# A per-row factor on VectorE: one operation with a scalar operand, or two multiplications of columns

## The chip, the cores and the metric

The kernel runs on one core of a Trainium2 chip. The metric is the time of one execution on the device, in microseconds (us), lower being better. Engines are named as in the profile: PE (TensorE), with its weight loads as PEld, DVE (VectorE), ACT (ScalarE), POOL (GpSimd) and SP (the engine that issues most transfers).

## The reference, cut to what matters

One encoder layer on 1024 tokens of width 1024: a combined projection, differential attention and a state-space mixer side by side, an output projection with a layer norm, and a mixture of 32 experts with a second layer norm. The change touches the differential attention alone. Each of its 4 heads has two softmax distributions over the same keys, and the second is taken from the first with a factor:

```python
sc = jnp.einsum('bqhcd,bkhcd->bhcqk', qi, k).astype(jnp.float32) * scale
p = jax.nn.softmax(sc, axis=-1)
attn = p[:, :, 0] - lam * p[:, :, 1]
return jnp.einsum('bhqk,bkhe->bqhe', attn.astype(v.dtype), v)
```

Then follow a root-mean-square norm over each head's 128 outputs and a gain.

## The kernel before, in words

**Stages.** The first stage makes the projections (line 244) beside the state-space mixer (`ssm_prepare`, `ssm_unit`). The second is attention, a loop over 32 units; woven into it are the gate of the mixer (`glu`, line 733), the splitting of the output weights (`wo_part`, line 877) and, at its end, preparations for routing. The third is the output projection (`mix`, line 1077) over 8 blocks of 128 tokens, with the layer norm (`layernorm`) and routing (`route`). The fourth is the experts (lines 1237 and 1246), and the fifth the second norm.

**A unit of attention** is one head `h` and one block `i` of 128 queries; it has `n = 128 * (i + 1)` keys. `scores` (line 771) makes the two score matrices on PE (lines 780 and 781), masks 64 rows with a MEMSET (789 or 797), takes the negated maximum `nm` with a reduction on DVE (790 or 798), and forms the exponentials `p` on ACT with their sums into `L` (783). `L` has two columns for a unit, one for each distribution. `weigh` (line 802) then takes the reciprocals `RL` of both sums (805), makes the column `rho` (807), which has one number for each query, and adds `rho` times the second distribution to the first, in place in `p` (808). PE transposes the result (814), ACT or DVE copies it to `half` (815), and PE multiplies it with the values (818). The first distribution's own normalizing factor cancels in the norm, up to its epsilon, and is put in by `normalize` (line 821) through small multiplications of `ss` with `RL` on DVE (830, 831 and 834, shown under helper line 158), a power on POOL (833) and a product on POOL (835).

**The order of work.** The loop starts unit `u + 2` before it weighs unit `u`. Up to the first gather of the experts, a planner puts the traced instructions in order for each engine by its own estimates of when they are ready, so DVE's queue is not in the order of the code: reductions of a later unit stand between the steps of an earlier one. From that gather on (`pins`, line 1387) `keep_order` keeps each engine's order as traced. Each engine runs its own queue strictly in order. The tile `rho` comes from `sm` (line 754), which has four buffers of one column.

**What POOL does meanwhile.** It subtracts the rounded part of a tensor from the tensor, in pieces of 64 or 128 partitions by 1024 with two operands (the `split` helper's line 155; `queries`, line 764), for `ql`, `zl`, `wgl` and `wol`; it scales the gate (line 738, shown as helper line 170, on `wg_raw`); and it runs the power and the product of `normalize`.

**Helpers.** Many DVE instructions are recorded under the line of a helper: `mul` is 158, `sub` 155, `stt` (scalar_tensor_tensor, one operation with a scalar operand and a second one with a tensor) 164, and `ts` (tensor_scalar) 168 or 170. `nlam`, a column of 128 equal numbers, is made once, early (lines 408 to 410).

Of the kernel before, what the change touches and what calls it, by code (L numbers as in the profile page):

```python
# [16 lines left out]
ALU = mybir.AluOpType  # L17
# [97 lines left out]
def tile_kernel(ctx: ExitStack, tc: tile.TileContext, I: dict, out: bass.AP, dbg=None):  # L115
# [15 lines left out]
    def bank(name, which=0):  # L131

        if which == 1:
            turn[0] ^= 1
            which = 2 + turn[0]
        return psum.tile([P, 512], F32, tag=f"bank{which}", name=name, bufs=1 if which else 2)
# [20 lines left out]
    def mul(out_, a, b, eng=V):  # L157
        eng.tensor_tensor(out=out_, in0=a, in1=b, op=ALU.mult)  # L158
# [4 lines left out]
    def stt(out_, a, s, b, op0, op1):  # L163
        return V.scalar_tensor_tensor(out=out_, in0=a, scalar=s, in1=b, op0=op0, op1=op1)  # L164
# [243 lines left out]
    nlam = cp.tile([P, 1], F32, name="nlam")  # L408
# [345 lines left out]
    def sm(name, n, bufs=4):  # L754
        return cp.tile([P, n], F32, tag=name, name=name, bufs=bufs)
# [46 lines left out]
    def weigh(h, i, p_, L, RL, j, po):  # L802

        n = P * (i + 1)
        V.reciprocal(RL[:, j, :], L[:, j, :])
        rho = sm("rho", 1)
        stt(rho, L[:, j, 0:1], nlam, RL[:, j, 1:2], ALU.mult, ALU.mult)
        stt(p_[:, 0, 0:n], p_[:, 1, 0:n], rho, p_[:, 0, 0:n], ALU.mult, ALU.add)
        aT = half.get("aT", [8, P], bufs=2)
        for k0 in range(0, i + 1, 4):  # L810
            k1 = min(k0 + 4, i + 1)
            b_ = bank(f"at{h}_{i}_{k0}")
            for k in range(k0, k1):
                PE.transpose(b_[:, (k - k0) * P:(k - k0 + 1) * P], p_[:, 0, k * P:(k + 1) * P], ident)
            (V.tensor_copy if k0 else S.copy)(aT[:, k0:k1, :], b_[:, 0:(k1 - k0) * P].rearrange("p (k q) -> p k q", q=P))  # L815
        sl.put(p_)
        for k in range(i + 1):
            PE.matmul(po[:, j * P:(j + 1) * P], aT[:, k, :], vv[k // 4][:, k % 4, h * P:(h + 1) * P],  # L818
                      start=(k == 0), stop=(k == i))
# [74 lines left out]
    for u, (h, i) in enumerate(units):  # L894
        if u + LEAD < len(units):
            start(u + LEAD)
        L_, RL_, po_ = grp[h, i // 4]
        weigh(h, i, live.pop(u), L_, RL_, i % 4, po_)
        if u in late:
            late.pop(u)()  # L900
        ends[h, i // 4] = ends.get((h, i // 4), 0) + 1
        if ends[h, i // 4] == 4:
            late[u + LATE] = normalize(h, i // 4, po_, RL_)
        if u in fills:
            for f_, *a_ in fills[u]:
                {"ask": ask, "pre": glu_prepare, "glu": glu, "wo": wo_part}[f_](*a_)
        if u == ZERO:

            zero = sl.get([P, D], F32, "zero")
            G.memset(zero, 0.0)  # L910
            for j in range(4):
                SP.dma_start(moe_dram[512 * j:512 * j + 512, :].rearrange("(p a) n -> p a n", p=P),
                             zero.unsqueeze(1).broadcast_to([P, 4, D]))
# [703 lines left out]
```

## Time and profile before

| What | us |
|---|---|
| median of 3 runs | 1185.71 |
| lowest and highest of them | 1184.47, 1189.87 |
| the profiled execution, its own time | 1182.18 |
| its span in the trace | 1180.4 |
| DVE busy over the span | 970.2 |
| POOL busy over the span | 359.0 |

The span is the stretch between the first and the last instruction of the trace; 1.8 us of the profiled execution's own time lie around it. The profiled execution is 3.5 us below the median of the other runs, so a sum made on its rows is set against 1182.18 and then carried to the median.

To read the rows: a timeline row gives start, duration, engine, line, operation, the tile written and those read, shapes and a count; a duration reaches from the instruction's start on its engine to its end, so an instruction held up by something after it has started shows a long duration, not idle time. The chain of waits is the work that ended last, followed back from the end; a piece of it is the time that one group of instructions held the chain.

### The profile page before, as it was taken

Reading aid. Unit: us, or ns where it says so; the run is one execution under the profiler, and the core shown is the slowest. Engines: PE = TensorE matmul, PEld = TensorE weight load, DVE = VectorE, ACT = ScalarE, POOL = GpSimd, SP = SyncE. Lnnn points to the kernel's source line nnn. Section 1 sums busy time; section 2 is a strip of 40 time slices with the busy share of each in tenths; the row PEclk is TensorE's granted clock in tenths of the full one; section 3 lists DMA queues with packets and bytes.
Section 4 is the critical chain, followed back from the end, with each engine's and each line's share of the span. In section 5 each row is a group of like instructions: output and inputs, shape, how many; then the busy total and the mean of one; then the engine's idle time right before and its main releaser. Section 6 shows DMA issues by size and latency. Waiting matters only on the chain.

```text
span 1180.4 us, 15229 instructions
## 1 busy us (share of the span) xinstructions
PE 1081.9 (92%) x5345; PEld 902.0 (76%) x5345; DVE 970.2 (82%) x1430; ACT 711.6 (60%) x960; POOL 359.0 (30%) x297
## 2 busy tenths in 40 slices
PE   6979999896779899995999999999999999999983
PEld 4867887686668788884888888888888888888852
DVE  4898666657878874565999999999999999999955
ACT  3312333445656743213888888888888888888832
POOL 1087464422442643341212122122122122121122
PEclk9989999998999999995999999999999999999997
DMA  8531111211181454545699999999999999999582
GB/s 208 138 99 43 55 46 46 59 30 42 32 325 36 159 210 136 196 178 200 238 361 378 383 369 399 383 385 396 381 374 376 377 370 386 395 386 386 172 208 108
DMA packets 90622, 278.90 MB, mean 236 GB/s; under 512 B 29404, under 2 KB 49900, under 8 KB 66096
## 3 DMA queue, kind: packets, MB, share of 16 engines
q1 hardware_dynamic: 78016, 252.78, 57.1%
q0 software_dynamic: 11520, 24.83, 7.7%
q8 instruction: 43, 0.70, 0.2%
q10 hardware_dynamic: 1008, 0.30, 0.1%
q14 instruction: 35, 0.29, 0.1%
HBM read 254.12 MB, written 34.60 MB: 245 GB/s over the span
## 4 chain that ended last, share of the span: by engine, by line
PE 74%; DVE 13%; ACT 5%; DMA 3%; issue 3%; SPq 1%; POOL 1%; ACTq 0%; DVEq 0%; POOLq 0%
PE g L1246 15%; PE u L1246 14%; PE y L1237 14%; PE proj L244 8%; PE mix L1077 7%; PE xT L1207 3%; DMA misc<-in_w_in_dram 2%; ACT p L783 2%; PE glu L733 2%; PE po L818 1%; PE hT L1219 1%; PE x L1449 1%; PE pl L1099 1%; DVE ssmt L158 1%; DVE ssm L158 1%
## 5 line engine op out<-in xcount | busy, mean ns | idle before, releaser
L1146 POOL DMA_INDIRECT moe_dram<-yo,idx x30 | 52.1, 1738 | 425.9 <-DVE yo L164 425.9
L244 PE MATMUL proj<-xh,wa 128*128 128x512 f32 x256 | 75.9, 403 | 1.7 <-ACT ssm L678 1.6
L244 PE MATMUL proj<-xh,wb 128*128 128x512 f32 x256 | 73.9, 400 | 1.6 <-ACT ssm L678 1.6
L1077 PE MATMUL mix<-woh,mx 128*128 128x512 f32 x256 | 74.3, 401 | 0.7 <-ACT p L783 0.7
L1141 POOL DMA_INDIRECT gx<-h_dram,idx x32 | 60.2, 1881 | 22.5 <-DVE WT L161 13.1
L783 ACT ACTIVATE p<-s,nm 128x1024 f32<-128x1024 f32 (+7 forms) x64 | 47.3, 745 | 26.8 <-DVE nm L798 17.0
L244 PEld LDWEIGHTS proj<-xh,wa 128*128 128x128 f32 x256 | 48.6, 193 | 11.8 <-ACT ssm L678 1.8
L244 PEld LDWEIGHTS proj<-xh,wb 128*128 128x128 f32 x256 | 48.0, 191 | 11.4 <-ACT ssm L678 1.8
L1077 PEld LDWEIGHTS mix<-woh,mx 128*128 128x128 f32 x256 | 48.1, 191 | 10.5 <-ACT p L783 1.0
L1253 ACT ACTIVATE yo<-y,WT 128x1024 f32<-128x1024 f32 (+1 forms) x33 | 36.0, 1091 | 24.4 <-PE y L1237 24.4
L780 PE MATMUL s<-kk,qh 128*128 128x512 f32 (+3 forms) x96 | 38.0, 399 | 12.5 <-ACT p L783 12.2
L818 PE MATMUL po<-vv,half 128*128 128x128 f32 x288 | 43.4, 294 | 6.7 <-ACT half L815 6.6
L818 PEld LDWEIGHTS po<-vv,half 128*128 128x128 f32 x288 | 39.2, 205 | 9.9 <-ACT half L815 8.7
L1207 PEld LDWEIGHTS xT<-ident,gx 128*128 128x128 f32 x256 | 36.2, 208 | 9.9 <-DMA gx<-h_dram,idx 5.8
L1207 PE MATMUL xT<-ident,gx 128*128 128x128 f32 x256 | 36.9, 287 | 7.0 <-DMA gx<-h_dram,idx 5.6
L155 DVE TENSOR_TENSOR xe<-xT,xe 128x1024 fp32r<-128x1024 f32 (+1 forms) x33 | 39.2, 1189 | 4.3 <-ACT xe L174 4.3
L244 PE MATMUL proj<-xl,wa 128*128 128x512 f32 x128 | 42.6, 404 | 0.0
L164 DVE SCALAR_TENSOR_TENSOR yo<-gx,first,yo 128x1024 f32<-128x1024 f32 (+1 forms) x33 | 41.3, 1252 | 1.5
L1077 PE MATMUL mix<-wol,mx 128*128 128x512 f32 x128 | 42.2, 398 | 0.0
L244 PE MATMUL proj<-xl,wb 128*128 128x512 f32 x128 | 41.4, 399 | 0.0
L174 ACT CAST xe<-xT 128x1024 fp32r<-128x1024 f32 (+1 forms) x33 | 32.3, 979 | 13.6 <-PE xT L1207 13.6
L164 DVE SCALAR_TENSOR_TENSOR p<-p,rho 128x1024 f32<-128x1024 f32 (+7 forms) x32 | 36.2, 1135 | 1.0 <-DMA moe_dram<-zero 0.3
(864 smaller groups left out, 3546.7 us busy)
## 6 DMA issues: line engine op xcount, KB each, us to landing
misc<-in_w_in_dram SPq DMA_DIRECT2D x16, 512.0 KB, 3.9
moe_dram<-zero SPq DMA_DIRECT2D x4, 2048.0 KB, 13.2
xr<-in_x_dram SPq DMA_DIRECT2D x8, 512.0 KB, 8.5
wo_raw<-in_w_out_dram SPq DMA_DIRECT2D x4, 1024.0 KB, 4.8
xa<-in_x_dram SPq DMA_DIRECT2D x8, 512.0 KB, 3.5
h_dram<-xa SPq DMA_DIRECT2D x8, 512.0 KB, 3.2
mo<-moe_dram SPq DMA_DIRECT2D x8, 512.0 KB, 6.0
mo<-moe_dram POOLq DMA_DIRECT2D x8, 512.0 KB, 13.1
```

Of the source, the lines that this page charges most:

```text
L155: eng.tensor_tensor(out=out_, in0=a, in1=b, op=ALU.subtract)
L164: return V.scalar_tensor_tensor(out=out_, in0=a, scalar=s, in1=b, op0=op0, op1=op1)
L244: PE.matmul(o[:, hs], wt[kt // 4][:, w_, kt % 4, :], x_[:, hs], start=(kt == 0 and n == 0), stop=(kt == KT - 1 and n == 2))
L780: PE.matmul(s_[:, c0:c0 + w], qd[0][:, c, tk], kk[h][:, c, c0:c0 + w], start=True, stop=False)
L783: S.activation(p_[:, c, 0:n], s_[:, 0:n], AF.Exp, bias=nm[:, c:c + 1], accum_out=L[:, j, c:c + 1])
L818: PE.matmul(po[:, j * P:(j + 1) * P], aT[:, k, :], vv[k // 4][:, k % 4, h * P:(h + 1) * P], start=(k == 0), stop=(k == i))
L1077: PE.matmul(o[-(hs.start > 0)][:, hs], mx[:, m_, kt, :], (woh, wol)[w_][kt // 2][:, kt % 2, hs], start=(kt == 0 and n == 0), stop=(kt == K ...
L1141: return G.indirect_dma_start(out=dst, out_offset=None, in_=h_dram[:, :], in_offset=bass.IndirectOffsetOnAxis(ap=ix, axis=0), bounds_check ...
L1146: G.indirect_dma_start(out=moe_dram[:, :], out_offset=bass.IndirectOffsetOnAxis(ap=ix, axis=0), in_=src, in_offset=None, bounds_check=2 * ...
L1207: PE.transpose(b_[:, kt * P:(kt + 1) * P], rows(g_, kt), ident)
L1237: PE.matmul(y[h_], hid[e][:, x_, kt, :], w_[:, k, HALVES[h_]], start=(kt == 0 and n == 0), stop=(kt == 3 and n == 2))
L1246: PE.matmul(o, xT[e][:, x_, kt, :], w_[:, k, :], start=(kt == 0 and n == 0), stop=(kt == KT - 1 and n == 2))
```

## The change

The factor `rho = L0 * nlam * RL1` of each unit was one scalar_tensor_tensor on DVE, which takes the column `L0`, multiplies it with the scalar operand `nlam` and then with the column `RL1`. It becomes two tensor_tensor multiplications, the second in place and dependent on the first. Nothing else is edited; the loop runs it 32 times.

```diff
         V.reciprocal(RL[:, j, :], L[:, j, :])
         rho = sm("rho", 1)
-        stt(rho, L[:, j, 0:1], nlam, RL[:, j, 1:2], ALU.mult, ALU.mult)
+        mul(rho, L[:, j, 0:1], RL[:, j, 1:2])
+        mul(rho, rho, nlam)
         stt(p_[:, 0, 0:n], p_[:, 1, 0:n], rho, p_[:, 0, 0:n], ALU.mult, ALU.add)
```

## Rows read from the trace of the kernel before

**Rows 1.** Windows: stretch, length; busy us (instructions) of PE, PEld, DVE, ACT, POOL; clock, DMA.

```profile
262.00:425.00 163.00, 134.45 (x790) 116.30 (x789) 133.41 (x260) 102.01 (x214) 69.53 (x53) 0.93 0.36 123
425.00:1180.00 755.00, 715.58 (x3381) 592.25 (x3379) 654.31 (x775) 521.93 (x605) 173.13 (x138) 0.98 0.83 315
```

**Rows 2.** Chain of waits from 262 to 450 us, shares by line.

```profile
by line: PE mix L1077 17.6%; ACT p L783 10.9%; PE glu L733 10.1%; PE po L818 8.7%; PE s L780 6.4%; issue 5.7%; DVE p L164 5.7%; PE s L781 5.2%; DVE nm L798 4.2%; DVE rho L164 4.0%; PE at L814 3.3%; ACT half L815 2.9%; DVE nm L790 2.1%; ACT 
```

**Rows 3.** Chain of waits in order of time, pieces: start us, us, what.

```profile
276.26 0.07 DVE rho L164
...
312.58 2.63 DVE rho L164
...
315.23 3.17 DVE p L164
```

**Rows 4.** Groups of DVE instructions by line, attention: count, busy us and mean ns.

```profile
L164 DVE SCALAR_TENSOR_TENSOR rho<-L,nlam,RL 128x1 f32<-128x1 f32 x32 | 13.8, 434 | 0.6
...
L158 DVE TENSOR_TENSOR ss<-ss,RL 128x4 f32<-128x4 f32 x18 | 3.1, 175 | 1.2 <-POOL ss L833 1.2
```

**Rows 5.** Timeline of DVE: an undisturbed unit, and two small multiplications.

```profile
307.46 0.22 DVE L158 TENSOR_TENSOR ss<-ss,RL 128x4 f32<-128x4 f32 x2
...
319.56 0.15 DVE L805 RECIPROCAL RL<-L 128x2 f32<-128x2 f32 x1
319.75 0.22 DVE L164 SCALAR_TENSOR_TENSOR rho<-L,nlam,RL 128x1 f32<-128x1 f32 x1
320.01 0.48 DVE L164 SCALAR_TENSOR_TENSOR p<-p,rho 128x256 f32<-128x256 f32 x1
```

**Rows 6.** Waits between engines in attention: total us, times, longest.

```profile
ACT p L783 <- DVE nm L798: 17.0, 10, 3.7
...
PE at L814 <- DVE p L164: 3.8, 2, 2.6
```

**Rows 7.** Timelines of POOL and DVE around 372 us, and an undisturbed scaling.

```profile
361.86 0.62 POOL L170 TENSOR_SCALAR wg_raw<-wg_raw 128x512 f32<-128x512 f32 x1 [9.56 <-ACT wg_raw L737]
...
370.23 4.84 POOL L155 TENSOR_TENSOR zl<-zT,zh 128x1024 fp32r<-128x1024 f32 x2 [0.72 <-PE at L814]
375.05 1.32 POOL L170 TENSOR_SCALAR wg_raw<-wg_raw 128x512 f32<-128x512 f32 x1
```

```profile
371.89 0.87 DVE L164 SCALAR_TENSOR_TENSOR rho<-L,nlam,RL 128x1 f32<-128x1 f32 x1
372.79 3.10 DVE L164 SCALAR_TENSOR_TENSOR p<-p,rho 128x768 f32<-128x768 f32 x1
...
376.04 0.82 DVE L798 TENSOR_REDUCE nm<-s 128x1 f32<-128x640 f32 x1
```

**Rows 8.** Timeline of DVE and POOL at the end of attention.

```profile
406.22 4.74 POOL L155 TENSOR_TENSOR wol<-wo_raw,woh 128x1024 fp32r<-128x1024 f32 x2 [0.59 <-ACT woh L174]
...
408.27 0.40 DVE L164 SCALAR_TENSOR_TENSOR rho<-L,nlam,RL 128x1 f32<-128x1 f32 x1
...
408.77 2.46 DVE L164 SCALAR_TENSOR_TENSOR p<-p,rho 128x256 f32<-128x256 f32 x1
...
410.90 0.20 POOL L970 MEMSET route<- 128x128 bf16 x1
411.07 4.70 POOL L155 TENSOR_TENSOR wol<-wo_raw,woh 128x1024 fp32r<-128x1024 f32 x2
411.16 2.34 DVE L168 TENSOR_SCALAR route<-iof 128x32 f32<-128x32 f32 x1
...
413.82 0.42 DVE L790 TENSOR_REDUCE nm<-s 128x2 f32<-128x256 f32 x1
...
416.19 5.06 POOL L155 TENSOR_TENSOR wol<-wo_raw,woh 128x1024 fp32r<-128x1024 f32 x2
```

**Rows 9.** Chain of waits, pieces at the start of the output projection and of the experts.

```profile
415.14 7.26 PE mix L1077 x23
...
545.17 4.43 DMA gx<-h_dram,idx
```

## The prediction

> **What bounds the kernel now.** I read the busy times by stage first. In attention, 163 us long, PE and DVE are each busy for some 134 us, neither of them throughout; behind it PE is busy for 716 of 755 us [rows 1]. So attention is the stage in which DVE can set the end, and what is lost there is carried on: from 415 us the chain of waits runs on PE's output projection, then over routing and the gather of tokens into the experts [rows 9]; I find no idle stretch that would give a loss back.
>
> Next the chain of waits between 262 and 450 us, by line. It changes hands all the time; `rho` holds 4.0% of it, 7.5 us of 188 [rows 2]. In order of time `rho` stands there in 7 of the 32 units, at 276, 280, 288, 313, 333, 372 and 408 us; the first is a piece of 0.07 us, the longest of 2.63 us [rows 3]. That spread is the point. Undisturbed, `rho` takes 0.22 us [rows 5], yet the mean over 32 is 434 ns [rows 4]: 32 x (0.434 - 0.22) = 6.8 us of its 13.8 us are waiting that shows as duration.
>
> What it waits for is seen when DVE and POOL are laid beside each other. From 370.23 us POOL runs two subtractions with two operands, 4.84 us in all, so 2.42 us each. `rho` starts at 371.89 and ends at 372.76, when the first is over; `p` starts at 372.79 and ends 3.10 us later, after the second is over at about 375.07 [rows 7]. Around 408 us the same pair of steps meets the same kind of pair [rows 8]. So an instruction of DVE with two operands that comes during such a subtraction is held until it ends, gets through at the seam, and the next one on DVE is held by the next subtraction.
>
> **The change, step by step.** Removed: 32 scalar_tensor_tensor on one column. Added: 64 tensor_tensor on one column. No transfer, semaphore of another engine or buffer is added, and POOL, ACT and PE issue what they issued.
>
> *The plain cost.* From `rho`'s start to `p`'s it is 0.26 us (319.75 to 320.01), and from `RL`'s start to its dependent `rho` 0.19 us for an instruction of 0.15 us [rows 5]. The nearest row for a small multiplication is `ss`, 18 of mean 175 ns, about 0.15 us where nothing holds it [rows 4]. A dependent one should then take 0.19 us from start to start, as after `RL`, so two take 0.38 in place of 0.26: **+0.12 us a unit**. Lower bound: two `ss` multiplications that do not need each other take 0.22 us together [rows 5], so 0.22 in place of 0.26, -0.04. Upper bound: each multiplication as dear as the old `rho`, 0.52 in place of 0.26, +0.26. I take +0.12, since the second multiplication does need the first. Over the 7 units on the chain that is 0.8 us (bounds -0.3 and +1.8). For the other 25 I take nothing: what covers it is that `p` is made ahead of need, as PE's transposes waited for `p` only twice in the stage [rows 6]. Without that cover it would be 25 x 0.12 = 3.0 us.
>
> [...] With 32 x 0.12 us on the path everywhere that would be 3.8 us; the chain, with 7 units, gives 0.8.
>
> *One more seam.* Where POOL runs two subtractions in a row, `rho` now passes the first seam as its first multiplication, the second multiplication is held in `p`'s place, and `p` comes after the pair. That alone costs little, as `p` had to wait for the end of the pair anyway. It costs where POOL has something next. The chain has two such places.
> - At 375.05 the scaling of `wg_raw` is next. It took 1.32 us because `p` was ahead of it; by itself it takes 0.62 [rows 7]. Now the second multiplication takes that seam and the scaling comes before `p`. **+0.6 us**, bounds 0 (`p` still slips in ahead) and 0.62. Queued behind `p` on DVE are a mask and `nm` of the next unit, for which ACT waits.
> - At 408 us POOL runs six subtractions, with only a MEMSET of 0.20 us at 410.90 between the second and the third, which starts at 411.07 [rows 8]. Now the first multiplication passes at about 408.6, the second at about 410.95, and `p` is ready 0.19 us later, at 411.14: 0.07 us after the third has begun. `p` is then held for 4.70 / 2 = **2.35 us**. Behind it on DVE stand the TENSOR_SCALAR on `iof`, which in the trace of before is held for one subtraction too (2.34 us), and then `nm` at 413.82; ACT's exponentials wait for that, and PE's first output projection at 415.14 for those [rows 8, 9]. Everything there moves by one subtraction. Bounds 0 (the 0.07 us go the other way) and 4.7 (`iof` misses a further seam).
>
> The other contacts (288, 308, 313 and 333 us) have a pause or a transfer of POOL's behind the pair, and one at 389 us lies off the chain: nothing but the plain cost.
>
> The sum is 0.8 + 0.6 + 2.4 = 3.8 us, bounds -0.3 and 1.8 + 0.6 + 4.7 = 7.1. The profiled execution would go from 1182.18 to 1186.0, and the median, 3.5 us above it, from 1185.71 to **1189.5**. That is +0.32%, below the 0.5% (5.9 us) that a measurement of this kernel can tell from no change.
>
> [...]
>
> **The rivals.**
> - *Hidden.* `p` gets in before the third subtraction. For it: a margin of 0.07 us, worked out from starts in one execution. Against it: `p` cannot start before the second multiplication is done, and POOL needs nobody. Time: 0.8 + 0.6 = 1.4, so 1187.1.
> - *Slower: a further seam missed.* Place: the six subtractions from 406.22 us, where DVE's queue holds `p`, `iof` and then the subtractions for the output projection. Each two-operand step that shifts behind one more of POOL's costs 2.35 us. It decides once one more than forecast is missed on the chain: 3.8 + 2.35 = 6.2 us, 1191.9; with two 1194.2, with three 1196.6. For it: POOL runs back to back there. Against it: only three of the six are left by then, and POOL's work isn't made longer, so later steps find it idle sooner.
> - *Faster: the planner's order changes.* It orders DVE by estimates, and the extra step leaves it a gap between the two multiplications, or before `p`. If it puts the next unit's `nm` there, which does not read what POOL holds, ACT gets on while `rho` and `p` would be held. For it: ACT waited 17.0 us for `nm` in 10 waits [rows 6], and at 372 us `nm` came 4.15 us after `rho` had started [rows 7], at 313 us it was 2.63 + 3.17 us of the chain [rows 3]. Both together give -9.9 + 1.4 = -8.5, so 1177.2; one of them only stays within 0.5%. Against it: the planner need not know of POOL's hold, and `nm` was not put there where a gap was open before.
> - *The change does nothing.* If the two multiplications overlapped as freely as the `ss` pair, 0.22 for 0.26 us, the sum is between -0.3 and 0: 1185.7. They are dependent, so this is a small part of the hidden case.
>
> **How the numbers follow.** Chances: forecast 0.36; hidden, with no cost at all among it, 0.24; slower 0.26, as an order that shifts can add holds as well as take them away; faster 0.14. The first two lie within 0.5%: faster 0.14, same 0.60, slower 0.26. The range takes in the forecast, the hidden case and the slower one up to three missed seams (1196.6), and at its low end the sum's lower bound with one of the two gains of the faster case (1185.71 - 0.3 - 4.15 = 1181.3): **1181 to 1197**. Left out are two gains at once and worse orders.
>
> **What would show it.** Right: two TENSOR_TENSOR on `rho` for each unit, about 0.15 us each and 0.19 us apart where POOL is idle; DVE with 32 instructions more; where POOL subtracts in pairs, the long durations sit on both multiplications and `p` is short; at the end of attention `p` is held once more, and the first output projection starts about 3.8 us later. Wrong: `nm` in other places between the steps, an output projection that starts earlier or at the same time, or a difference that arises behind 425 us, where nothing was edited.

## The result, and the profile after

The changed kernel takes 1193.15 us (median of 20 runs, 1188.99 to 1195.74); the kernel before, run beside it, 1184.85 us (20 runs). The ratio is 1.0066 with an interval of 1.0055 to 1.0077, so the change costs **7.8 us**. Forecast were 3.8 us, which would have lain below the 0.5% at which the prediction draws the line for "same" (0.60 of its chances); the measured 0.66% is "slower", which had 0.26. The profiled execution after took 1190.73 us, its span is 1189.0 us.

The windows by stage of the kernel after, to be read beside [rows 1] (stretch, length, busy us and instructions of PE, PEld, DVE, ACT, POOL, clock, DMA):

```profile
262.00:425.00 163.00, 127.81 (x755) 109.01 (x754) 130.29 (x277) 97.33 (x200) 67.27 (x51) 0.92 0.34 111
425.00:1180.00 755.00, 725.38 (x3423) 600.25 (x3421) 655.28 (x792) 526.37 (x620) 178.31 (x140) 0.98 0.84 317
```

Up to 425 us PE has done 35 instructions fewer than before (755 for 790) and ACT 14 fewer; they now lie behind 425 us. Two pieces of the chain of waits, in order of time, answer to [rows 9]:

```profile
426.24 6.08 PE mix L1078 x20
...
552.56 4.36 DMA gx<-h_dram,idx
```

The output projection starts 11.1 us later than at 415.14, the first gather 7.4 us later than at 545.17, and the end of the span is 8.6 us later, so 3.7 us are won back between projection and gather, and behind the gather 1.2 us are added (635.2 us to the end before, 636.4 after). The first unit's `p` starts at 274.65 before and at 275.69 after, so 1.0 of these lay ahead of the first `p`. **First `p` to first gather** is the measure used for all runs below: 270.52 us before, 276.87 after, +6.4.

Groups of DVE instructions by line of the kernel after (count, busy us, mean ns), beside [rows 4]:

```profile
L158 DVE TENSOR_TENSOR rho<-L,RL 128x1 f32<-128x1 f32 x32 | 12.3, 386 | 0.6
L158 DVE TENSOR_TENSOR zT<-zT,wg_raw 128x512 f32<-128x512 f32 x8 | 11.6, 1451 | 0.8 <-POOL wg_raw L170 0.7
L158 DVE TENSOR_TENSOR rho<-rho,nlam 128x1 f32<-128x1 f32 x32 | 7.1, 224 | 0.5
```

The same view of the kernel before has this for the products on `zT`:

```profile
L158 DVE TENSOR_TENSOR zT<-zT,wg_raw 128x512 f32<-128x512 f32 x8 | 5.4, 677 | 0.0
```

Two things are to be seen. The waiting on `rho` sits mostly on the first multiplication (386 ns in the mean for 0.16 us of work), little of it on the second (224 ns), where the forecast had it on both (in the old order, run 1 below, it is on both: 389 and 428 ns). And eight products that the diff does not touch now take 11.6 us instead of 5.4. Both come from one cause, as runs 1 and 2 below show: the planner has put the work in another order, up to the first gather. Against the trace of before, at least 15 instructions of POOL, 50 of ACT, 278 of PE and, beside the 32 new ones, 108 of DVE would have to be moved to get the new order. In 4 of the 32 units an `nm` now stands between the two multiplications, in none of run 1; the prediction had named that as a sign of being wrong. The pair of POOL's subtractions for `wgl`, before and after:

```profile
332.03 4.69 POOL L155 TENSOR_TENSOR wgl<-wg_raw,wgh 128x1024 fp32r<-128x1024 f32 x2
```

```profile
357.78 4.91 POOL L155 TENSOR_TENSOR wgl<-wg_raw,wgh 128x1024 fp32r<-128x1024 f32 x2 [6.04 <-ACT wgh L174]
```

The timeline of DVE where nothing is in the way shows the plain cost:

```profile
371.57 0.15 DVE L805 RECIPROCAL RL<-L 128x2 f32<-128x2 f32 x1
371.76 0.16 DVE L158 TENSOR_TENSOR rho<-L,RL 128x1 f32<-128x1 f32 x1
371.96 0.16 DVE L158 TENSOR_TENSOR rho<-rho,nlam 128x1 f32<-128x1 f32 x1
372.15 0.88 DVE L164 SCALAR_TENSOR_TENSOR p<-p,rho 128x640 f32<-128x640 f32 x1
```

From `RL` to `p` it is 0.58 us, against 0.45 in [rows 5]: +0.13 a unit, where 0.12 were forecast. The timelines of DVE and POOL at the end of attention answer to [rows 8]:

```profile
414.12 4.86 POOL L155 TENSOR_TENSOR wol<-wo_raw,woh 128x1024 fp32r<-128x1024 f32 x2 [0.65 <-ACT woh L174]
...
414.53 2.23 DVE L164 SCALAR_TENSOR_TENSOR p<-p,rho 128x256 f32<-128x256 f32 x1
416.69 2.84 DVE L158 TENSOR_TENSOR zT<-zT,wg_raw 128x512 f32<-128x512 f32 x1
...
419.09 2.64 POOL L155 TENSOR_TENSOR wol<-wo_raw,woh 128x1024 fp32r<-128x1024 f32 x1
...
419.64 2.11 DVE L158 TENSOR_TENSOR rho<-L,RL 128x1 f32<-128x1 f32 x1
421.69 0.29 POOL L972 TENSOR_SCALAR_AFFINE_SELECT route<-route 128x128 bf16<-128x128 bf16 x1
421.78 0.21 DVE L158 TENSOR_TENSOR rho<-rho,nlam 128x1 f32<-128x1 f32 x1
...
421.96 2.33 POOL L155 TENSOR_TENSOR wol<-wo_raw,woh 128x1024 fp32r<-128x1024 f32 x1
...
422.09 2.48 DVE L164 SCALAR_TENSOR_TENSOR p<-p,rho 128x256 f32<-128x256 f32 x1
```

DVE is held here four times running: `p` of one unit, a product on `zT` that stood earlier in the kernel before, the next unit's first multiplication, and its `p`. The second multiplication (0.21 us) slips through between two subtractions, beside a short instruction of POOL's own (0.29 us). So the place that the forecast had priced is not in this kernel any more; others have come.

### The profile page after: what moved, and what is told of

Same layout as the page of the kernel before. It is cut to its first block, busy times and chain, and to the rows that moved or that the text cites. A ratio compares the mean times of both kernels' runs of the same rounds, so it can differ in the third digit from the quotient of the medians.

```text
span 1189.0 us, 15265 instructions
## 1 busy us (share of the span) xinstructions
PE 1086.8 (91%) x5345; PEld 904.0 (76%) x5345; DVE 966.7 (81%) x1462; ACT 710.7 (60%) x960; POOL 359.1 (30%) x297
## 4 chain that ended last, share of the span: by engine, by line
PE 63%; DVE 5%; issue 2%; ACT 2%; DMA 0%; POOL 0%; DVEq 0%; ACTq 0%; POOLq 0%
PE g L1247 15%; PE u L1247 14%; PE y L1238 14%; PE mix L1078 8%; PE xT L1208 3%; PE glu L733 2%; PE po L819 1%; PE hT L1220 1%; PE x L1450 1%; PE pl L1100 1%; PE s L780 1%; PE x L1460 1%; DVE rho L158 1%; PE x L1456 1%; PE at L815 1%
## 5 line engine op out<-in xcount | busy, mean ns | idle before, releaser
L155 DVE TENSOR_TENSOR xe<-xT,xe 128x1024 fp32r<-128x1024 f32 (+1 forms) x33 | 39.1, 1184 | 4.2 <-ACT xe L174 4.2
L780 PEld LDWEIGHTS s<-kk,qh 128*128 128x128 f32 x96 | 20.5, 213 | 28.8 <-ACT p L783 26.1
```

What stands on the lines that cost most here:

```text
L155: eng.tensor_tensor(out=out_, in0=a, in1=b, op=ALU.subtract)
L780: PE.matmul(s_[:, c0:c0 + w], qd[0][:, c, tk], kk[h][:, c, c0:c0 + w], start=True, stop=False)
```

## The experiments

The change does two things at once: it makes `rho` in another way, and it gives the planner another program to order. The experiments take these apart. To hold an order, `keep_order` gives each engine, from the first traced instruction on, the sequence that the planner had made for another kernel; neighbours get a dependency that makes no wait. Every difference from that sequence is named. The core of that edit, shortened and not repeated below (there the second multiplication is written out as the instruction that `mul` or `ts` makes, so that it can be put behind the first):

```diff
-        for i in traced[at:]:
-            tc.add_manual_dep(i, prev[i.engine].name,
+        for e, mine in traced.items():
+            row = [mine[k] for k in planned[e]]
+            for a, b in zip(row, row[1:]):
+                tc.add_manual_dep(b, a.name,
...
```

The kernel after and all twelve runs; "net" is the change in the stretch from the first `p` to the first gather, from one profile each:

| rho | order | ratio to before | interval | net us |
|---|---|---|---|---|
| two tensor_tensor (the change) | planned | 1.0066 | 1.0055 to 1.0077 | +6.4 |
| 1: two tensor_tensor | old | 1.0071 | 1.0050 to 1.0091 | +7.3 |
| 2: one scalar_tensor_tensor | that of after | 1.0073 | 1.0049 to 1.0098 | +8.6 |
| 3: one tensor_scalar | old | 0.9965 | 0.9948 to 0.9981 | -3.2 |
| 4: one tensor_scalar | planned | 1.0048 | 1.0031 to 1.0064 | +6.6 |
| 5: two tensor_scalar | old | 0.9954 | 0.9934 to 0.9974 | -3.7 |
| 6: one tensor_scalar | that of after | 1.0012 | 0.9995 to 1.0029 | +1.4 |
| 7: two tensor_tensor, factors swapped | planned | 1.0060 | 1.0036 to 1.0085 | +7.3 |
| 8: one tensor_scalar | POOL old, rest planned | 0.9980 | 0.9959 to 1.0001 | +0.3 |
| 9: two tensor_tensor in units 0 to 15 | old | 1.0024 | 1.0004 to 1.0043 | +3.8 |
| 10: two tensor_tensor in units 16 to 23 | old | 1.0011 | 0.9993 to 1.0029 | -0.3 |
| 11: two tensor_tensor in units 24 to 31 | old | 1.0024 | 1.0007 to 1.0042 | +3.8 |
| 12: one tensor_scalar | DVE old, rest planned | 0.9987 | 0.9971 to 1.0002 | +0.1 |

One per cent is 11.8 us. The net follows the ratio within some 3 us everywhere, so what the kernels differ in arises in attention and on the way to the first gather.

### 1. The two multiplications in the old order

```diff
-        stt(rho, L[:, j, 0:1], nlam, RL[:, j, 1:2], ALU.mult, ALU.mult)
+        mul(rho, L[:, j, 0:1], RL[:, j, 1:2])
+        mul(rho, rho, nlam)
```

> The two multiplications of the changed kernel, with every engine's instructions held in the order of the kernel before (the second multiplication right behind the first). Theory A, the planner's new order makes the loss: the ratio is 1.000 to 1.003 (0 to +3.8 us, the plain cost and the seam at the end of attention at most), and POOL's and PE's stretches start where they did before. Theory B, the added operation itself makes it, by its cost and by one more hold behind POOL's subtractions: 1.005 to 1.008, as in the changed kernel. In the trace both expect the first output projection later than 415 us: A by 0 to 4 us, B by 6 us or more.

Measured: 1192.31 us (12 runs), 1.0071. That is in the range of theory B, and the first output projection starts at 422.01 us, 6.9 later than before, as B had it. The operation alone, with the order unchanged, gives the whole loss, about 8.4 us by the ratio. Since every other instruction stands where it stood, the two traces can be laid on each other, and the lateness of each `nm` against that of before tells where time goes. This run was 0.43 us ahead at the first `p`. The steps from there:

| up to the `nm` that starts before at | late by | step | what lies there |
|---|---|---|---|
| 311.63 | +0.37 | 0.80 | the plain cost, unit by unit |
| 337.96 | +1.00 | 0.63 | contacts at 320 to 338 us |
| 370.98 | +2.00 | 1.00 | PE slow at 340 to 345 us, granted clock 0.69 for 1.00 |
| 376.04 | +2.59 | 0.59 | the scaling of `wg_raw` gets in ahead of `p` |
| 385.67 | +4.21 | 1.62 | PE slow at 380 to 385 us, granted clock 0.66 for 1.00 |
| 405.62 | +4.45 | 0.24 | contact at 393 us |
| 413.82 | +6.87 | 2.42 | one more subtraction at the end of attention |

Together 7.30 us. The last step is the forecast's. The timelines of DVE and POOL in this run:

```profile
413.14 2.27 DVE L808 TENSOR_TENSOR rho<-rho,nlam 128x1 f32<-128x1 f32 x1
...
415.33 0.21 POOL L971 MEMSET route<- 128x128 bf16 x1
415.50 4.84 POOL L155 TENSOR_TENSOR wol<-wo_raw,woh 128x1024 fp32r<-128x1024 f32 x2
...
415.51 2.61 DVE L164 SCALAR_TENSOR_TENSOR p<-p,rho 128x256 f32<-128x256 f32 x1
...
420.69 0.42 DVE L790 TENSOR_REDUCE nm<-s 128x2 f32<-128x256 f32 x1
```

The second multiplication takes the seam that `p` had before, and `p` comes 0.01 us after the third subtraction has begun. The margin of 0.01 us is that of one execution. What the forecast did not have is the two stretches of a slower PE; runs 9 to 11 show below that such stretches come and go without the program.

### 2. The one operation in the new order

```diff
-        mul(rho, L[:, j, 0:1], RL[:, j, 1:2])
-        mul(rho, rho, nlam)
+        stt(rho, L[:, j, 0:1], nlam, RL[:, j, 1:2], ALU.mult, ALU.mult)
```

Every engine in the order of the kernel after; `rho` stands where the second multiplication stood.

> The one scalar_tensor_tensor of the kernel before, at the place of the second multiplication, with every engine's instructions held in the order of the changed kernel. Theory A (order): slower than before by 4 to 8 us, ratio 1.003 to 1.007, and the first output projection starts at 422 to 426 us as in the changed kernel. Theory B (operation): ratio 0.999 to 1.002, first output projection before 418 us.

Measured: 1193.13 us (6 runs), 1.0073, and the first output projection at 424.71 us: theory A this time. So the new order alone, with the old operation, gives the whole loss too. The two causes do not add: with both the ratio is 1.0066. The eight products on `zT` take 11.6 us as in the kernel after, and PE's scores wait for ACT at the same three places between 348 and 357 us. In these rows the granted clock of the kernel after between 350 and 360 us stands beside that of before (windows, columns as above):

```profile
350.00:360.00 10.00, 6.62 (x21) 5.03 (x21) 8.32 (x19) 5.96 (x10) 3.59 (x3) 0.52 0.03 8
```

```profile
350.00:360.00 10.00, 9.76 (x63) 8.67 (x62) 6.65 (x13) 3.95 (x7) 1.73 (x3) 1.00 0.01 2
```

PE gets through 21 instructions instead of 63. In the run with the one operation the clock is 0.52 there as well.

### 3 and 4. One tensor_scalar, in the old order and planned

```diff
-        stt(rho, L[:, j, 0:1], nlam, RL[:, j, 1:2], ALU.mult, ALU.mult)
+        ts(rho, L[:, j, 0:1], nlam, ALU.mult, RL[:, j, 1:2], ALU.mult)
```

The product is the same, but of its operands only `L0` is a tensor; `nlam` and `RL1` are scalar operands, one for each partition. In run 3 each engine has the order of the kernel before, in run 4 the planner is free.

> The factor made by one tensor_scalar that takes the column L0 as its only tensor and nlam and RL1 as scalar operands, in the order of the kernel before. If what DVE waits for is a second operand read from the same memory while POOL subtracts, this rho is held nowhere: 0.15 to 0.25 us in all 32 units, and p takes the first seam in its place, so that p ends one subtraction (2.4 us) earlier at 313, 333, 372 and 408 us; ratio 0.992 to 0.998. If any DVE instruction that comes during a subtraction is held, rho shows the same long durations as before and the ratio is 0.999 to 1.001.

> The same tensor_scalar, with the planner left to choose the order. DVE has as many instructions as before. If only the operation mattered, the time is that of the same work in the old order, within 0.2%. If the order is a lottery in which a small change of an estimate moves the whole of attention, it differs from that by 0.3% or more, in either direction.

Measured: 1181.1 us (12 runs), 0.9965, and 1191.21 us (10 runs), 1.0048. The group of `rho` in run 3:

```profile
L170 DVE TENSOR_SCALAR rho<-L,nlam,RL 128x1 f32<-128x1 f32 x32 | 8.4, 265 | 0.7
```

By itself the instruction is dearer than the old one (0.27 us for 0.22), yet no instance of the 32 is longer than 0.28 us, where the old one had up to 2.62. **It is never held.** The kernel gets faster by 4.1 us, inside the expected range. The gain lies in fewer places than expected: the `nm` behind comes 2.41 us earlier at 313 us and 1.41 at 372, of which 0.61 are gone at the `nm` after, but 0.16 at 333 and nothing at 408. And the same 32 instructions under a free planner cost 10 us more than in the old order: here the order is worth more than the operation.

### 5. Two tensor_scalar in the old order

```diff
-        stt(rho, L[:, j, 0:1], nlam, RL[:, j, 1:2], ALU.mult, ALU.mult)
+        ts(rho, L[:, j, 0:1], RL[:, j, 1:2], ALU.mult)
+        ts(rho, rho, nlam, ALU.mult)
```

> Two multiplications in each unit, as in the change, but each a tensor_scalar with one column as its tensor and one column as a scalar operand (L0 by RL1, then rho by nlam). Every engine in the order of the kernel before. So there are as many operations as in the change, one needing the other, yet none of them has a second tensor operand. Theory (what costs is that a second instruction with two tensor operands stands between rho and p and is held by POOL's subtractions, with what follows from that): no rho is held, so none is longer than 0.4 us, p starts as early as with one tensor_scalar, and the time is 1179 to 1184, ratio 0.995 to 0.999. Rival (the number of operations and the need of the second for the first cost it): as the two tensor_tensor in the same order, 1190 to 1193, ratio 1.005 to 1.007.

Measured: 1179.64 us (9 runs), 0.9954. This is the change as it was meant, two multiplications with the second needing the first, in the same order as run 1, and it is 12.7 us faster than run 1 by the medians, 13.9 by the ratios, and faster than the kernel before. Its plain cost is the highest of all, for the two take 0.25 us each from start to start, 0.50 where the old operation took 0.26. So neither the number of operations nor the dependency costs anything that can be seen beside the holds. The timelines of DVE and POOL show why:

```profile
312.76 0.21 DVE L168 TENSOR_SCALAR rho<-L,RL 128x1 f32<-128x1 f32 x1
...
312.81 5.44 POOL L155 TENSOR_TENSOR ql<-qr,qh 64x1024 fp32r<-64x1024 f32 x2
...
313.01 0.21 DVE L808 TENSOR_SCALAR rho<-rho,nlam 128x1 f32<-128x1 f32 x1
313.26 2.74 DVE L164 SCALAR_TENSOR_TENSOR p<-p,rho 128x768 f32<-128x768 f32 x1
...
316.16 1.09 DVE L798 TENSOR_REDUCE nm<-s 128x1 f32<-128x896 f32 x1
```

The second multiplication runs in 0.21 us in the midst of POOL's subtraction. Only `p`, with two tensors, is held, once (2.74 us, for 1.02 where nothing holds it). Before, `rho` was held by the first subtraction and `p` by the second [rows 3], and the next `nm` came 2.40 us later, with the `nm` ahead at 311.63 us in both traces (row of before):

```profile
318.56 1.09 DVE L798 TENSOR_REDUCE nm<-s 128x1 f32<-128x896 f32 x1
```

At 372 us the same exchange gives another 1.40 us, of which 0.60 are gone at the `nm` after.

### 6. One tensor_scalar in the new order

The edit of run 3, with every engine in the order of the kernel after.

> rho as one tensor_scalar with two scalar operands (not held), every engine in the order of the kernel after. Theory (the new order costs by rho being held at other places): the time falls from 1193.1 by more than the 3.8 us that the same exchange gave in the old order, to 1184 to 1188. Rival (the new order costs by the products for zT and by p, which POOL's later subtractions hold, and by PE's waits with the lower clock behind them): zT and p stay as long as they were, PE's granted clock between 350 and 360 us stays below 0.7, and the time is 1189 to 1193, ratio 1.003 to 1.007.

Measured: 1187.08 us (12 runs), 1.0012. The expected range was 1184 to 1188 if holds on `rho` were what costs, 1189 to 1193 if not: the first. Against run 2, which has the same order, 6.1 thousandths are gone, some 7 us. Against run 3, which has the same operation, 4.7 thousandths stay, 5.6 us. These are the part of the new order that does not come from `rho`: the products on `zT` take 11.6 us as in run 2, and the granted clock between 350 and 360 us is 0.53, as it was expected to stay if the rival held. Both theories had a share.

### 7. The factors swapped, planned

```diff
-        mul(rho, L[:, j, 0:1], RL[:, j, 1:2])
-        mul(rho, rho, nlam)
+        mul(rho, L[:, j, 0:1], nlam)
+        mul(rho, rho, RL[:, j, 1:2])
```

> The two multiplications of the change with their factors swapped (nlam first, then RL1), the planner free. The work is that of the kernel after to the last instruction; the planner gives another order on each engine. Theory (orders of equal work lie some us apart, since the planner doesn't reckon with holding): the time differs from that of the kernel after by more than 2 us either way, within 1182 to 1198, and the first output projection starts earlier or later by as much. Rival (the work decides): 1192 to 1194, ratio 1.006 to 1.008, as with the change.

Measured: 1192.28 us (8 runs), 1.0060. The order is not that of the kernel after on any engine: at least 14 instructions of POOL, 111 of DVE and 317 of PE would have to be moved. It lies nearer to the order of before (4, 40 and 146), and the pair for `wgl` starts early, at 334.27 us. The time is that of the kernel after. This speaks for the rival, though it is only one more order: here the waiting is on the second multiplication too (464 ns in the mean), and the products on `zT` take 7.8 us.

### 8 and 12. One tensor_scalar, with one engine's order held

The edit of run 3; in run 8 POOL alone is held to the order of the kernel before, in run 12 DVE alone.

> rho as one tensor_scalar, POOL alone held to the order of the kernel before, the other engines as the planner puts them. With every engine in the old order the same work took 1181.1, with all of them planned 1191.2. Theory (the new orders cost by where POOL's subtractions stand: the wgl ones later, across the products for zT): 1181 to 1184, ratio 0.997 to 0.999. Rival (it is DVE's own order, or PE's and ACT's): 1188 to 1192, ratio 1.003 to 1.006.

> rho as one tensor_scalar, DVE alone held to the order of the kernel before, the other engines planned; the planner then puts POOL in the old order but for one instruction, ACT but for 7 and PE but for 36. With POOL alone held to the old order the time was 1184.8, with every engine held 1181.1, with none 1191.2. Theory (DVE's and POOL's orders together make the difference): 1180 to 1183, ratio 0.995 to 0.998. Rival (PE's order counts as well): 1184 to 1187, ratio 0.998 to 1.001.

Measured: 1184.79 us, 0.9980, and 1182.22 us, 0.9987 (12 runs each, in different groups, so the ratios are what compares; their intervals overlap). Run 8 is in the range of its theory. Run 12 is in that of its theory by the time alone; by the ratio it is in the rival's, so that PE's order may count as well, which its interval leaves open. Holding POOL's order takes away 6.8 of the 8.3 thousandths between run 4 and run 3. In run 12 the planner by itself puts POOL in the old order but for one instruction, and the result is no different. The products on `zT` take 7.6 us in run 8 and 5.4 in run 12, against 11.3 in run 4. So most of what the new order costs is gone once POOL's subtractions stand in their old places. That it is due to them alone is not shown: in run 8 DVE, PE and ACT got other orders again than in run 4.

### 9 to 11. The two multiplications in a part of the units

```diff
-        stt(rho, L[:, j, 0:1], nlam, RL[:, j, 1:2], ALU.mult, ALU.mult)
+        if u < 16:
+            mul(rho, L[:, j, 0:1], RL[:, j, 1:2])
+            mul(rho, rho, nlam)
+        else:
+            stt(rho, L[:, j, 0:1], nlam, RL[:, j, 1:2], ALU.mult, ALU.mult)
```

The condition is `16 <= u < 24` in run 10 and `u >= 24` in run 11; the order is the old one.

> The two multiplications in the first 16 of the 32 units (to about 343 us), the one operation in the other 16, every engine in the order of the kernel before. In the run with two multiplications everywhere, nm at 343.92 us came 1.95 us later than before, and PE's lower clock had just begun. Theory (the loss is a sum of contacts with POOL's subtractions at separate places): nm near 344 us and all behind it, the first output projection too, come 2.0 us later than in the profile of before; time +2.0, about 1186.9, ratio 1.002. Rival (the loss is made at the end of attention, where lateness is taken up again by waits): the first output projection within 0.7 us of that of before, ratio 1.000.

> The two multiplications in units 16 to 23 alone (about 343 to 389 us), the one operation elsewhere, every engine in the order of the kernel before. Theory (sum of contacts): the scaling of wg_raw slips in before p at 375 us, +0.5 to 0.6 us at the next nm; if PE's longer wait there lowers its clock as in the run with two multiplications everywhere, +2.1 us by nm at 389 us, and as much at the first output projection; time 1187, ratio 1.002. Rival (that clock fell only because the contacts ahead had already shifted the work): +0.6 us and a granted clock of 1.00 between 380 and 390 us, ratio 1.0005.

> The two multiplications in the last 8 units alone (from about 389 us), the one operation elsewhere, every engine in the order of the kernel before. Theory (sum of contacts, and the forecast's step for the end of attention): p of unit 29 is held by one more subtraction, 2.35 to 2.45 us; with 0.2 to 0.5 us from the contact at 389 us the first output projection starts 2.4 to 2.9 us later than before; time 1187.4, ratio 1.002. Rival (unit 29 reaches its seam in time when nothing ahead is late): under 0.7 us, ratio 1.000.

Measured: 1.0024, 1.0011 and 1.0024, together 1.0059 against 1.0071 in run 1, inside its interval. The loss adds up over places, as the theory had it, as far as intervals of some 0.002 to either side can tell. For run 10 alone the ratio lies between its theory and its rival; there the trace decides. The seam at 375 us in run 10, DVE and POOL:

```profile
374.27 2.30 DVE L809 TENSOR_TENSOR rho<-rho,nlam 128x1 f32<-128x1 f32 x1
...
376.52 0.62 POOL L170 TENSOR_SCALAR wg_raw<-wg_raw 128x512 f32<-128x512 f32 x1
...
376.60 1.34 DVE L164 SCALAR_TENSOR_TENSOR p<-p,rho 128x768 f32<-128x768 f32 x1
```

The scaling is ahead of `p`, and the next `nm` is late by 2.05 us after 1.47, so 0.58 us are lost: the forecast's second term. The lateness then stays at 2.0 to 2.2 us up to the last `nm` of attention: no loss to PE's clock, which is 1.00 from 380 to 390 us, as the rival of this run said. (Some 0.9 us are won back between there and the gather.) The end of attention in run 11, DVE and POOL:

```profile
415.01 2.12 DVE L158 TENSOR_TENSOR rho<-L,RL 128x1 f32<-128x1 f32 x1
417.17 0.16 DVE L809 TENSOR_TENSOR rho<-rho,nlam 128x1 f32<-128x1 f32 x1
...
417.23 4.83 POOL L155 TENSOR_TENSOR wol<-wo_raw,woh 128x1024 fp32r<-128x1024 f32 x2
...
417.43 2.42 DVE L164 SCALAR_TENSOR_TENSOR p<-p,rho 128x256 f32<-128x256 f32 x1
```

Here `p` is 0.20 us late for the seam; the lateness goes from 6.29 to 8.60 us, so this place costs 2.31 us, and 0.24 us come from the contact ahead of it, as in run 1. It is late by the length of the added multiplication, though here it is the first one that waits out a subtraction. Most of the rest of this profile's +3.8 net arose where the program is still that of before: the granted clock fell to 0.69 between 345 and 350 us, and the `nm` that before starts at 341.97 became 0.88 us later. That is the step of 1.00 us that run 1 has at the same `nm`. Run 9, which has run 1's program up to there, does not have it (5.31 us late ahead of it, 5.32 behind).

In run 9 the profile has a loss that run 1 has not, though the two kernels do not differ up to unit 16. The windows from 290 to 300 us, run 1 first, then run 9:

```profile
290.00:300.00 10.00, 7.74 (x54) 6.92 (x54) 9.29 (x26) 5.88 (x14) 0.84 (x2) 1.00 0.24 54
```

```profile
290.00:300.00 10.00, 7.48 (x32) 6.47 (x31) 7.57 (x18) 3.66 (x9) 1.80 (x3) 0.66 0.23 52
```

PE's waits there, in the same sequence:

```profile
291.24 0.85 PE L815 MATMUL at<-ident,p 128*128 128x128 f32 x6 [1.50 <-DVE s L797]
...
293.10 0.50 PE L780 MATMUL s<-kk,qh 128*128 128x512 f32 x1 [1.01 <-ACT p L783]
```

```profile
292.21 0.85 PE L818 MATMUL at<-ident,p 128*128 128x128 f32 x6 [1.50 <-DVE s L797]
...
294.07 0.79 PE L780 MATMUL s<-kk,qh 128*128 128x512 f32 x1 [1.02 <-ACT p L783]
```

In both PE waits 1.50 us and then 1.01 or 1.02 us; in one the granted clock is 1.00 over these 10 us and the next three matmuls of 128x512 on `s` take 0.39 or 0.40 us, in the other the clock is 0.66, they take 0.63 us each, and the lateness grows by some 2.4 us. Run 3's profile has a like step of 1.5 us in this stretch. So a single profile carries steps of this size that the program does not decide.

## Why the prediction was right, and where it was not

The sign and the range held, though the range is 16 us wide and the loss is twice the forecast. The terms that came out were those of a kernel that the change does not make, the two multiplications in the old order; for the kernel that it does make the range held by luck as much as by mechanism, and no run itemizes its 7.8 us.

**The plain cost** was right by the unit, +0.13 us for +0.12, but not in the count of units: the 0.80 us that the forecast had for all 7 units on the chain were there in the first third of run 1, where 3 of the 7 lie. It weighs little beside the holds, as run 5 shows, in which it is twice as large.

**The seam at 375 us** was right: 0.59 us in run 1 and 0.58 in run 10, for 0.6.

**The end of attention** was right: 2.42 us in run 1 and 2.31 in run 11, for 2.35, by the mechanism named, with the third subtraction 0.01 and 0.20 us ahead of `p` where 0.07 were worked out. So the hidden rival, which needed `p` ahead of it, was not the case in these two profiles; with 0.01 us it was near.

**"The other contacts … nothing but the plain cost"** was the first step that failed. Those at 320 to 338 us gave 0.63 us and that at 393 us 0.24. Small shifts bring other instructions into a subtraction: in run 1 a `p` that started at 327.15 us before, ahead of POOL, starts 0.06 us after it at 328.16 and is held for 2.43 us, most of which is won back at the next contact (rows of DVE before, then of POOL and DVE in run 1):

```profile
327.15 0.27 DVE L164 SCALAR_TENSOR_TENSOR p<-p,rho 128x128 f32<-128x128 f32 x1
```

```profile
328.10 4.72 POOL L155 TENSOR_TENSOR zl<-zT,zh 128x1024 fp32r<-128x1024 f32 x2 [2.99 <-ACT zh L174]
328.16 2.43 DVE L164 SCALAR_TENSOR_TENSOR p<-p,rho 128x128 f32<-128x128 f32 x1
```

**PE's clock** was not in the sum at all. In run 1 it makes 2.62 of 7.30 us. How much of that belongs to the operation is open: the step at 340 us is absent from run 9 with the same program and present in run 11 with the old one, and the step at 380 us is absent from run 10. On the average of all runs a lower clock does go with the two tensor_tensor: 0.9605 in the 12 of run 1 for 0.9648 in the 27 of before beside them, and 0.9666 in the 9 of run 5 for 0.9639 in the 28 of before beside those. Where it is lost these means do not show, and run 6 has 0.9608 at almost the time of before. Holds make PE wait longer (3.18 us at 338.87 in run 1, 2.56 at 337.86 before), but in these runs the length of a wait did not decide the clock. In run 1 a wait of 2.02 us was followed by a lower clock (0.66 from 380 to 385 us), in run 10 one of 2.04 us at the same place was not (1.00; rows of PE, run 1 first, then run 10):

```profile
380.49 0.68 PE L780 MATMUL s<-kk,qh 128*128 128x512 f32 x1 [2.02 <-ACT p L783]
```

```profile
379.95 0.50 PE L780 MATMUL s<-kk,qh 128*128 128x512 f32 x1 [2.04 <-ACT p L783]
```

**The order of work** was the second step that failed. The forecast had "the planner's order changes" as a way to be faster, with 0.14, and its sum took the old order as given. Run 2 shows that the new order alone costs as much as the operation alone, and with both the loss is no larger than with either. Of the signs that the prediction named, the waiting on both multiplications did not come, and the output projection starts 11.1 us later instead of 3.8. That the measured 7.8 us lie near the forecast of the slower rival, 6.2, has no meaning: its mechanism, one more missed subtraction among the last ones, was not what made it. Why the two do not add can be read from the end of attention: in the new order it is the first multiplication, like the old operation, that waits out a subtraction, and the second fits into the seam behind it. This is read from the rows and was not tried by itself.

**The gain of the faster rival** was right in place, not in size or cause. It had 5.8 us at 313 us and 4.15 at 372, from an `nm` put ahead of `p`; without the hold on `rho`, `nm` comes 2.40 and 1.40 us earlier (run 5). It took an operation that is not held, and the order that the planner did make was slower. `nm` itself was not held: the five that start inside a subtraction of POOL's in the trace of before take 0.42 to 1.21 us, as long as those of their shape elsewhere.

The whole, then: what an operation of one column costs here is not its duration but whether it has a second tensor among its operands. With one, POOL's subtractions held it for up to 2.62 us in the kernel before and 2.33 in the kernel after; without one it was not held in runs 3 and 5, where the longest of 32 took 0.28 us and the longest of 64 took 0.21. The TENSOR_SCALAR on `iof`, with 32 columns, was held for 2.34 us [rows 8], so it takes more than the name of the operation to tell. On one column, though, the operations with a second tensor are also those with another name than tensor_scalar; no run parts the two.

A version that beats both kernels is run 5, with run 3 close by: intervals of 0.9934 to 0.9974 and 0.9948 to 0.9981 against the kernel before. Both need the old order to be held; under a free planner one tensor_scalar is slower than the kernel before, and two were not tried there.

## What to carry to other kernels

Where GpSimd works on tensors beside VectorE, try small per-row factors in which only one operand is a tensor and the rest are scalar operands: here that was worth some 13 us between two forms of the same two multiplications. Where a planner orders the work by its own estimates, any edit gives another order, so measure the edit in a held order and the order with the old code before putting a price on either; here each gave the whole difference, and they did not add. A sum of small terms on one trace can be right in its largest terms and still too small, because late work meets other work, and because a stretch of a lower PE clock, which one execution has and the next has not, costs as much as such a term (1.00 and 1.62 us in run 1, at 0.69 and 0.66).

## What the runs showed of the hardware that was not expected

The scalar_tensor_tensor on one column, with a column as its second tensor, was held by POOL's subtractions for up to 2.62 us; a tensor_scalar with two columns as scalar operands did the same product in 0.27 us and was not held in any of 32 instances, nor was one with a single scalar operand at 0.21 us, 0.25 from start to start, in any of 64. A multiplication of two columns took 0.16 us where nothing held it, 0.19 to 0.20 from start to start when the next one needed it.

Two programs that do not differ up to that point, after the same waits of PE (1.50 and some 1.0 us), had a granted clock of 1.00 in one execution and 0.66 in another from 290 to 300 us, with some 2.4 us between them; runs of one kernel that differ by 7 us (1188.99 to 1195.74 for the kernel after) go with their mean granted clock, with a correlation of -0.69 over its 20 runs.
